# A diffusion-backbone layer on one core: TensorE in a hand-written, software-pipelined order from the step sums to the out-projection

## The chip, the cores and the metric

The kernel runs on one core of one Trainium2 chip. Its engines are PE (TensorE, matrix products), PEld (TensorE's weight load, which overlaps PE), DVE (VectorE), ACT (ScalarE), POOL (GpSimd) and SP (SyncE), which in this kernel only issues transfers. Each engine takes its instructions from a queue of its own, in order; semaphores hold an instruction back until what it reads is there. The metric is the device time of one execution in microseconds (us). A time "at 127.2" is counted from the start of the profiled span.

## The reference, cut to what matters

One layer over 256 noised tokens `x` and 256 context tokens `ctx`, both 1024 wide, float32 throughout. Both are normalised and modulated and go through one in-projection; the latent tokens pass a two-direction Mamba-2 scan that starts from the context's final state, and beside it a short gated convolution; both meet in the out-projection. A top-4-of-32 mixture of experts follows.

```python
mod_x = (jax.nn.silu(c) @ w_mod[i] + b_mod[i]).reshape(b, N_MOD, 1, D_MODEL)
hx = modulate(rmsnorm(x, norm1_g[i]), mod_x[:, 0], mod_x[:, 1])
proj = h @ w_in                                        # 1024 -> 5664 columns: z, x, B, C, dt, sc_b, sc_c, sc_u
xbc = jax.nn.silu(conv_seq(proj[..., X0:DT0], ssd_conv_w) + ssd_conv_b)
...
y, hf, hb = ssd_bidir(xs, bm, cm, dt_f, dt_b, a_f, a_b, d_skip, h0_f, h0_b)
y_ssd = group_rmsnorm(y.reshape(b, l, D_SSD) * jax.nn.silu(z), ssd_norm_g, SSD_GROUPS)
y_sc = sc_b * sc_conv(sc_c * sc_u, sc_conv_w)
out = jnp.concatenate([y_ssd, y_sc], axis=-1) @ w_out
...
x = x + mod_x[:, 2] * ox
x = x + mod_x[:, 5] * moe(modulate(rmsnorm(x, norm2_g[i]), mod_x[:, 3], mod_x[:, 4]), *moe_w)
```

`ssd_chunked` works in two chunks of 128 tokens: inside a chunk each head's output is (scores x decays) times the inputs, and the state carried in is added with its own decay.

## The kernel before, in words

**Numbers.** A float32 product is made from a high and a low part of each factor, both in the type fp32r: `split` copies the high part on ACT (`hi`) and subtracts for the low part (`lo`) on DVE or POOL, and `gemm` issues three products per row block of 128 (lines L292, L293, L295). A block of `proj` has 24 matmuls, 512 columns wide where latent and context tokens go together (X), 256 wide for the latent tokens alone (C, SC, SU, SB, Z). Each pair of blocks has one weight tile of 1 MB, which `load_cols` fetches (L223, tiles `wiX`, `wiC`, ...) into a ring of three slots (`RA`).

**Stages.** Up to 60 us: modulation of phase 0, norms, transposes, the B block and the first X blocks. Then:

- 60 to 127 us: the X blocks (2 to 7) and the C blocks, each followed by a depthwise convolution and SiLU on ACT and DVE. Beside them the step sums: `pds` (PE), then on DVE `dtx`, the running sums `acs` and `wc` (L431 to L453). `pc` (L460) turns these to token order, six small transposes, and DVE copies them into `dtc`. `px` (L501) transposes each X block, and DVE multiplies with `dtc` into `xdt` and `ws`. `decay_rows` splits the sums into the rows of `a4` on DVE (L487, L489). The four context states `pst` (L535), copied by ACT into `h0`, and the scores `pcb` (L544) end the stage.
- 127 to 187 us: the scan, 16 steps (8 head pairs `hp`, 2 directions `d_`). A step makes two decay tiles `rb` in PSUM (L565, L568; two buffers), ACT takes three exponentials of each (L572 to L576), DVE multiplies by the scores (`mx`), POOL by C (`ex`), and PE adds six products into `py` (L583, L586, L590), a tile of 64 output columns per head.
- 187 to 284 us: the short-conv blocks SC, SU, SB (24) and the gate blocks Z (8).
- 284 to 341 us: the out-projection, 192 matmuls (L825 to L827) into four PSUM tiles `po`; its weights `wo` are split on the way into `oh` and `ol`. `group_norm` (POOL, L671) makes the gated and normed `y` that the last half of the products needs. Then the router and, to the end, the 32 experts, whose weights (`gu`, `dn`, 1 MB a transfer, 384 of them) pass through 17 slots: `ringa` (3), `ringm` (2), `ringb` (5), six more, and one of another tile.

**Modulation on the side.** Phases 1 and 2 (`m1`, `m2`) are generators of 8 small steps (`pmod`, L202: one 1 MB tile `wm` against the conditioning vector, four products side by side in 32-column tiles of the array) and a final part of 16 tiny and 2 wide products (`pq`, `pgate`, L210, L216). Their tiles pass through `ringm`, two slots (`RM`).

**Order.** The program is written with a tile framework. A scheduler that works from modelled costs sets each engine's order, and so PE's; the code's order only fixes what depends on what. `tc.issue_after` holds an instruction behind another one.

Of the kernel before, what the change touches and what calls it, by code (L numbers as in the profile page):

```python
# [8 lines left out]
F32 = mybir.dt.float32  # L9
# [53 lines left out]
def body(ctx, tc, x, ctx_in, vectors_in, w_mod, b_mod, w_in, w_out, w_router, b_router, w_gate_up, b_gate_up,  # L63
# [128 lines left out]
    def mods(ph, gate, gate_first, col):  # L192
# [6 lines left out]
        for k in range(KD):  # L199
            w = load_mod(ph, k)  # L200
            for j in range(4):
                nc.tensor.matmul(acc[32 * j:32 * j + 32, :], ct[:, k, :], w[:, 512 * j:512 * j + 512],  # L202
                                 start=(k == 0), stop=(k == KD - 1), skip_group_check=True)
            yield
        nc.vector.tensor_add(rows, rows, acc)
# [196 lines left out]
    nc.tensor.matmul(pds, sdt.rearrange("p d h -> p (d h)"), dq, start=True, stop=True)  # L402
    se.close()

# [3 lines left out]
    for g in range(2):  # L408
        pp = pps[g]
        b = t2a.tile([P, 2, T], F32, name=f"b{g}")  # L410
        conv_silu(pp, 8 + g, 512, b)
        pb = ps.tile([P, 512], F32, tag="misc", bufs=2, name=f"pb{g}")
        for i in range(NT):
            nc.tensor.transpose(pb[:, i * P:(i + 1) * P], b[:, 1, i * P:(i + 1) * P], ident)
        nc.vector.tensor_copy(bcT[:, :, g, :], pb[:, :T].rearrange("p (i n) -> p i n", i=NT))
        bch.append(b)
# [40 lines left out]
    pc = ps.tile([P, 512], F32, tag="misc", bufs=2, name="pc")  # L457
    for i in range(NT):
        for w_, src in enumerate((dtx[:, :T], wc, acs)):
            nc.tensor.transpose(pc[:, (w_ * 2 + i) * 64:(w_ * 2 + i + 1) * 64], src[:, i * P:(i + 1) * P],  # L460
                                ident[0:H2, 0:H2])
    dtc = t2a.tile([P, 3, NT, 64], F32, name="dtc")
    nc.vector.tensor_copy(dtc[:, 0:2], pc[:, 0:256].rearrange("p (a b c) -> p a b c", a=2, b=2))
    steps_done = nc.vector.tensor_scalar(dtc[:, 2], pc[:, 256:384].rearrange("p (b c) -> p b c", b=2), -1.0, None, op0=ALU.mult)
# [27 lines left out]
    for q in range(4):  # L492
        wv = load_cols(X0 + 256 * q, f"X{q}") if q else None
        for half in range(2):
            ti = 2 * q + half
            pp = proj(wv, half, 512, f"X{ti}", nc.gpsimd) if q else pps[2 + half]
            cx = t2a.tile([P, 512], F32, tag="cx", bufs=2, name=f"cx{ti}")
            conv_silu(pp, ti, 512, cx.rearrange("p (m t) -> p m t", m=2), weighted.ins if ti else None)
            px = ps.tile([P, 512], F32, tag="misc", bufs=2, name=f"px{ti}")
            for i in range(4):  # L500
                nc.tensor.transpose(px[:, i * P:(i + 1) * P], cx[:, i * P:(i + 1) * P], ident)  # L501
            nc.gpsimd.tensor_scalar(yb[:, ti, :], cx[:, :T], vec("d", ti), None, op0=ALU.mult)

            for s_, dst in enumerate((xdt, ws)):
                for i in range(NT):
                    nc.vector.tensor_mul(
                        dst[:, :, i, 2 * ti:2 * ti + 2, :],
                        dtc[:, s_, i].rearrange("p (d h) -> p d h", d=2)[:, :, 2 * ti:2 * ti + 2, None]
                        .to_broadcast([P, 2, 2, HD]),
                        px[:, (2 * s_ + i) * P:(2 * s_ + i + 1) * P].rearrange("p (h q) -> p h q", h=2)[:, None]  # L510
                        .to_broadcast([P, 2, 2, HD]))
            if ti == 1:
                decay_rows()
            if ti >= 4:
                with tc.issue_after(steps_done.ins):
                    next(m1)


    t2s = sa.enter_context(tc.tile_pool(name="t2s", bufs=1, reuse_waits="tile"))
    cch = []  # L520
    wv = load_cols(C0, "C")
    for g in range(2):
        pp = proj(wv, g, T, f"C{g}")
        cc = t2s.tile([P, T], F32, name=f"c{g}")
        last_silu = conv_silu(pp, 10 + g, T, cc[:, None, :])
        cch.append(cc)
# [4 lines left out]
    for g in range(2):  # L531
        for d_ in range(2):
            pst = ps.tile([P, 512], F32, tag="misc", bufs=2, name=f"pst{d_}{g}")
            for i in range(NT):
                nc.tensor.matmul(pst, bcT[:, i, g, :], ws[:, d_, i, 8 * g:8 * g + 8, :],  # L535
                                 start=(i == 0), stop=(i == NT - 1))
            nc.scalar.copy(h0[d_][g], pst)


    cb = [[None, None], [None, None]]  # L540
    for g in range(2):
# [12 lines left out]
    for hp in range(8):  # L554
        py = ps.tile([P, T], F32, tag="py", bufs=1, name=f"py{hp}")
        g = hp // 4
        for d_ in range(2):
            ja, jb = (0, 1) if d_ == 0 else (1, 0)
            half = slice(P, T) if d_ == 0 else slice(0, P)
            xd = xdt[:, d_]  # L560
            mxs, exs = [], []
            for h_ in (2 * hp, 2 * hp + 1):
                row = 32 * d_ + h_
                pr = ps.tile([P, 4, P], F32, tag="rb", bufs=2, name=f"rb{h_}_{d_}")
                nc.tensor.matmul(pr, selr[:, row:row + 1].to_broadcast([P, P]), a4, start=True, stop=False,  # L565
                                 skip_group_check=True)
                for blk in (0, 2) if d_ == 0 else (1, 2):
                    nc.tensor.matmul(pr[:, blk, :], identb, maskf if d_ == 0 else maskb, start=False,  # L568
                                     stop=(blk == 2), skip_group_check=True)
                mx = t2s.tile([P, 384], F32, tag="mx", bufs=4, name=f"mx{h_}_{d_}")  # L570
                with tc.issue_after(last_silu):
                    nc.scalar.activation(mx[:, 0:256], pr[:, 0:2, :].rearrange("p a b -> p (a b)"), AF.Exp,  # L572
                                         bias=dtc[:, 2, ja, row:row + 1])
                    nc.scalar.activation(mx[:, 256:384], pr[:, 2, :], AF.Exp, bias=dtc[:, 2, jb, row:row + 1])
                    ex = t2s.tile([P, 2, P], F32, tag="ex", bufs=4, name=f"ex{h_}_{d_}")
                    nc.scalar.activation(ex, pr[:, 3:0:-2, :] if d_ == 0 else pr[:, 0:4:3, :], AF.Exp)  # L576
                nc.vector.tensor_mul(mx, mx, cb[g][d_])
                exf = ex.rearrange("p a b -> p (a b)")
                nc.gpsimd.tensor_tensor(exf, exf, cch[g], op=ALU.mult)
                mxs.append(mx)  # L580
                exs.append(exf)
            for hh in range(2):
                nc.tensor.matmul(py[64 * hh:64 * hh + 64, :], xd[:, ja, 2 * hp + hh, :], mxs[hh][:, 0:256],  # L583
                                 start=(d_ == 0), stop=False, skip_group_check=True)
# [778 lines left out]
```

## Time and profile before

| | before |
|---|---|
| median of 3 runs | 1318.14 us (1315.64 to 1318.76) |
| the profiled execution's own time | 1318.35 us |
| its span | 1316.6 us |
| PE busy | 1186.5 us, 90% of the span |
| PEld, DVE, ACT, POOL busy | 41%, 33%, 20%, 11% |
| mean granted clock of PE | 0.963 |
| moved by DMA | 466 MB |

The profiled execution has 1.75 us outside the span that the trace covers. PE's busy share counts matmuls as they lie in its pipeline, so it does not tell how tightly they follow each other; for that the starts of successive matmuls are read.

### The profile page before, as it was taken

How to read it: one execution, taken by the hardware profiler on the slowest of the kernel's cores; microseconds unless marked ns; L12 is line 12 of the kernel's file. 1: busy time of each engine (PE TensorE's matmuls, PEld its weight loads, DVE VectorE, ACT ScalarE, POOL GpSimd, SP SyncE). 2: the span in 40 equal slices, each digit the busy share in tenths (PEclk: the TensorE clock that was granted, in tenths of full speed). 3: DMA queues.
4: the chain of work that ended last, by engine and by line, in shares of the span. 5: the costliest groups of instructions: out<-in, count | busy, mean ns of one | idle time of the engine just before them, and what ended most of it. 6: DMA issues, size and time to landing. Idle time of an engine off the chain costs nothing.

```text
span 1316.6 us, 16133 instructions
## 1 busy us (share of the span) xinstructions
PE 1186.5 (90%) x6105; PEld 543.7 (41%) x6105; DVE 428.9 (33%) x874; ACT 259.1 (20%) x509; POOL 139.0 (11%) x147
## 2 busy tenths in 40 slices
PE   7989999999899988899988879998987899888984
PEld 6666479977633332244223213432321243223221
DVE  5475344553523432222223212222321213212222
ACT  5445454435410010010001001000100010001002
POOL 1232454405300100000000000000000000000001
PEclk9989999999899999999999978999998999899997
DMA  9725439785599999999999999999999999999994
GB/s 324 258 96 160 160 94 318 233 327 209 217 371 416 416 416 415 415 415 416 417 417 415 416 416 417 417 416 414 415 416 417 416 417 416 416 417 417 416 416 161
DMA packets 111841, 466.12 MB, mean 354 GB/s; under 512 B 9576, under 2 KB 40424, under 8 KB 76944
## 3 DMA queue, kind: packets, MB, share of 16 engines
q1 hardware_dynamic: 111504, 464.37, 88.9%
q8 instruction: 50, 0.82, 0.3%
q0 software_dynamic: 256, 0.67, 0.1%
q14 instruction: 31, 0.25, 0.1%
HBM read 463.97 MB, written 1.05 MB: 353 GB/s over the span
## 4 chain that ended last, share of the span: by engine, by line
PE 57%; DMA 12%; DVE 6%; ACT 1%; issue 1%; POOL 0%; ACTq 0%; DVEq 0%; SPq 0%; POOLq 0%
PE pdn L1051 8%; DMA gu<-in_w_gate_up_dram 8%; PE pg L1039 7%; PE pl L1039 6%; PE pg L1109 6%; PE pc L1015 6%; PE pgl L1080 5%; DMA dn<-in_w_down_dram 5%; PE pdn L1093 4%; PE pdn L1116 3%; PE pd L927 2%; PE pgl L1074 1%; PE pat L1008 1%; DVE ye L1062 1%; PE po L827 1%; PE po L825 1%
## 5 line engine op out<-in xcount | busy, mean ns | idle before, releaser
L1039 PE MATMUL pg<-gu,xe 128*64 128x512 f32 x480 | 151.0, 603 | 2.2 <-DMA gu<-in_w_gate_up_dram 2.0
L1039 PE MATMUL pl<-gu,xe 128*64 128x512 f32 x480 | 148.0, 593 | 0.0
L982 ACT ACTIVATE s<-a 128x512 f32<-128x512 f32 (+1 forms) x35 | 19.1, 545 | 589.6 <-DVE a L981 589.6
L1080 PE MATMUL pgl<-gu,xe 128*32 128x512 f32 x896 | 115.9, 622 | 15.3 <-DMA gu<-in_w_gate_up_dram 15.3
L1015 PE MATMUL pc<-ye,gt 64*128 64x512 f32 (+1 forms) x256 | 101.5, 640 | 28.7 <-DVE ye L1062 14.7
L1051 PE MATMUL pdn<-dn,at 128*64 128x512 f32 x480 | 118.5, 640 | 6.9 <-ACT at L1010 6.8
L1017 DVE TENSOR_TENSOR x<-x,pc 128x512 f32<-128x512 f32 x128 | 84.4, 685 | 119.4 <-PE pc L1015 119.4
L981 DVE TENSOR_SCALAR a<-pg 128x512 f32<-128x512 f32 x21 | 14.5, 691 | 217.3 <-PE pg L1039 151.8
L1109 PE MATMUL pg<-gu,xe 128*128 128x512 f32 x192 | 83.9, 592 | 0.0
L1231 POOL DMA_DIRECT2D fg<-in_final_g_dram x1 | 0.6, 591 | 746.6 <-PE pd L927 746.6
L1015 PEld LDWEIGHTS pc<-ye,gt 64*128 64x128 f32 (+1 forms) x256 | 29.2, 185 | 101.1 <-DVE x L1017 45.5
L1093 PE MATMUL pdn<-dn,at 128*32 128x512 f32 x448 | 65.7, 696 | 5.4 <-ACT at L1010 5.4
L1062 DVE TENSOR_TENSOR ye<-g2s,pdn 128x512 f32<-128x512 f32 x29 | 19.9, 688 | 154.4 <-PE pdn L1051 107.6
L1039 PEld LDWEIGHTS pl<-gu,xe 128*64 128x64 f32 x480 | 41.8, 137 | 65.8 <-issue 65.5
L1039 PEld LDWEIGHTS pg<-gu,xe 128*64 128x64 f32 x480 | 38.2, 136 | 71.2 <-issue 57.4
L1051 PEld LDWEIGHTS pdn<-dn,at 128*64 128x64 f32 x480 | 34.2, 146 | 73.7 <-issue 57.6
L1080 PEld LDWEIGHTS pgl<-gu,xe 128*32 128x32 f32 x896 | 24.7, 111 | 91.4 <-issue 50.0
L1109 PEld LDWEIGHTS pg<-gu,xe 128*128 128x128 f32 x192 | 35.8, 190 | 41.6 <-issue 40.9
L927 PE MATMUL pd<-oh,hr 128*128 128x256 f32 (+1 forms) x256 | 41.9, 305 | 5.6 <-DVE xe L929 5.0
L1116 PE MATMUL pdn<-dn,at 128*128 128x512 f32 x96 | 43.5, 601 | 0.0
L927 PEld LDWEIGHTS pd<-oh,hr 128*128 128x128 f32 x256 | 34.1, 198 | 20.9 <-DVE xe L929 10.7
L995 DVE TENSOR_SCALAR go<-io,gp 128x128 f32<-128x128 f32 x56 | 18.6, 370 | 68.9 <-PE pgo L999 68.9
(398 smaller groups left out, 1678.7 us busy)
## 6 DMA issues: line engine op xcount, KB each, us to landing
gu<-in_w_gate_up_dram SPq DMA_DIRECT2D x256, 1024.0 KB, 19.9
dn<-in_w_down_dram SPq DMA_DIRECT2D x127, 1024.0 KB, 20.0
wm<-in_w_mod_dram SPq DMA_DIRECT2D x16, 1024.0 KB, 5.0
wim<-in_w_mod_dram SPq DMA_DIRECT2D x8, 1024.0 KB, 11.6
wo<-in_w_out_dram SPq DMA_DIRECT2D x8, 1024.0 KB, 6.9
wiX<-in_w_in_dram SPq DMA_DIRECT2D x4, 1024.0 KB, 10.6
wiSC<-in_w_in_dram SPq DMA_DIRECT2D x4, 1024.0 KB, 8.0
wiSU<-in_w_in_dram SPq DMA_DIRECT2D x4, 1024.0 KB, 6.4
```

The source lines that it names most:

```text
L927: nc.tensor.matmul(pd[:, :width], hr[n // 2][:, n % 2, k * P:(k + 1) * P], oh[:, n % 2, :], start=(n == 0), stop=(n == 3))
L982: nc.scalar.activation(s, a, AF.Sigmoid, scale=ALPHA)
L995: nc.vector.tensor_scalar(go if cap == P else go.rearrange("p (a s) -> p a s", s=cap), io1 if cap == P else io1[:, None, 0:cap].to_broadca ...
L1015: nc.tensor.matmul(pc_, lhs, rhs, start=True, stop=True)
L1017: return nc.vector.tensor_add(ysl, ysl, pc_).ins
L1039: nc.tensor.matmul(pp[64 * hf:64 * hf + 64, :], xk[k], gu[k][:, i * FF + hf * 512:i * FF + hf * 512 + 512], start=False, stop=(k == KD - 1 ...
L1051: down = nc.tensor.matmul(pdn[64 * hf:64 * hf + 64, :], at[:, kk % 4, 64 * (kk // 4):64 * (kk // 4) + 64], dn[kk // 2][:, (kk % 2) * D + h ...
L1062: nc.vector.tensor_mul(ye, g2s, pdn)
L1080: nc.tensor.matmul(pgl[32 * q:32 * q + 32, :], xk[k], gv[:, :, 256 * q:256 * q + 256], start=False, stop=(k == KD - 1), skip_group_check=True)
L1093: down = nc.tensor.matmul(pdn[j:j + 32, :], at[:, c2, 32 * q:32 * q + 32], dn[q][:, c2 * D + hf * 512:c2 * D + hf * 512 + 512], start=(q = ...
L1109: nc.tensor.matmul(pgs[i][hf], xk[k], gu[k][:, i * FF + hf * 512:i * FF + hf * 512 + 512], start=False, stop=(k == KD - 1))
L1116: nc.tensor.matmul(pdn, ats[kk // 4][:, kk % 4, :], dn[kk // 2][:, (kk % 2) * D + hf * 512:(kk % 2) * D + hf * 512 + 512], start=(kk == 0) ...
```

## The change: what it does

PE's order from `pds` to the last matmul of the out-projection is taken from the code (`tc.manual_schedule` for this one engine); the other engines' orders are still set by the scheduler. The code is cut into functions, and a written sequence calls them.

```diff
+    in_order = ExitStack()
+    in_order.enter_context(tc.manual_schedule(engines={mybir.EngineType.PE}))
+    with tc.issue_after(last[0]):
+        nc.tensor.matmul(pds, sdt.rearrange("p d h -> p (d h)"), dq, start=True, stop=True)
...
+    def c_block(g):
+        if g == 0:
+            wcol["C"] = load_cols(C0, "C")
+        pp = proj(wcol["C"], g, T, f"C{g}", nc.vector)
...
+    x_block(0)
+    x_block(1)
+    x_block(2)
+    context_b(0)
+    context_b(1)
+    x_block(3)
+    c_block(0)
+    for _ in range(3):
+        next(m1)
+    token_steps()
+    x_tokens(0)
+    x_tokens(1)
+    decay_rows()
+    c_block(1)
+    x_block(4)
+    x_tokens(2)
+    x_tokens(3)
+    x_block(5)
+    x_tokens(4)
+    for d_ in range(2):
+        context_state(d_, 0)
+    x_block(6)
+    x_tokens(5)
+    scores(0)
+    last_silu = x_block(7)
+    x_tokens(6)
+    scores(1)
+    for _ in range(2):
+        next(m1)
+    x_tokens(7)
+    sc_steps = [(kind, 2 * q + half) for q in range(4) for kind in "CUB" for half in range(2)]
+    fill = [lambda: context_state(0, 1), lambda: context_state(1, 1)]
+    fill += [lambda a=a: sc_block(*a) for a in sc_steps[:12]]
+    step = decays(0)
+    for s_ in range(16):
+        if fill:
+            fill.pop(0)()
+        if s_ >= 2:
+            next(m1 if s_ < 6 else m2, None)
+        done_ = step
+        if s_ < 15:
+            step = decays(s_ + 1)
+        outputs(s_, *done_)
...
+    sc_parts()
+    for a in sc_steps[12:]:
+        sc_block(*a)
+        sc_parts()
...
-        if n_ in (1, 2):
-            group_norm(n_ - 1, rgs[n_ - 1])
-        if n_ == 3:
+        if n_ in (2, 3):
+            group_norm(n_ - 2, rgs[n_ - 2])
+        if n_ == 4:
             bgr = router_operands()
...
+    in_order.close()
```

`token_steps` is the old code of `pc` and `dtc`, `x_tokens` that of `px`, `xdt` and `ws`, `context_state` that of one `pst`, `scores` that of one `pcb`, `decays` and `outputs` are the two halves of a scan step, and `sc_block` is one SC, SU or SB block. The products themselves stay as they were. The low parts of C1 and of the odd SU blocks move from POOL to DVE. In a generator's last step the addition of `pmod` to `rows` now stands before the yield. Transfers change their order on SP with all this; the two loads of `x2` (L806), which stood ahead of three weight transfers late in the out-projection, now follow all of `wo` and `gu0`.

Three places of the engines' orders follow; a name with a number behind its last underscore is one buffer, and "x8" stands for eight alike. The first place is PE around `pc`, the transposes of the step sums. Before, they stand inside block X4:

```order
L295 MATMUL ppX3_726<-hhi_188,loX3_723 128x512 x8
L292 MATMUL ppX4_773<-hhi_188,hiX4_769 128x512
L293 MATMUL ppX4_773<-hlo_189,hiX4_769 128x512
L292 MATMUL ppX4_773<-hhi_188,hiX4_769 128x512
L460 MATMUL pc_613<-ident_82,wc_604 128x64
L460 MATMUL pc_613<-ident_82,acs_603 128x64
L460 MATMUL pc_613<-ident_82,dtx_585 128x64
...
L293 MATMUL ppX4_773<-hlo_189,hiX4_769 128x512
```

After the change they stand behind the first C block and three steps of modulation phase 1 (`wm1_0` to `wm1_2`):

```order
L296 MATMUL ppC0_725<-hhi_188,loC0_722 128x256 x8
L202 MATMUL pmod1_756<-wm1_0_760,ct_169 32x512 x4
L202 MATMUL pmod1_756<-wm1_1_766,ct_169 32x512 x4
L202 MATMUL pmod1_756<-wm1_2_772,ct_169 32x512 x4
L470 MATMUL pc_778<-ident_82,dtx_582 128x64
L470 MATMUL pc_778<-ident_82,wc_601 128x64
L470 MATMUL pc_778<-ident_82,acs_600 128x64
```

What moved: a whole block and three modulation steps now stand between X3 and `pc`, and nothing of X4 stands before it.

The second place is PE in the scan. Before, a step's products into `py1` (heads 2 and 3, forward) lie split around the next step's decay tiles `rb2_1` and `rb3_1` and one quarter of a modulation step:

```order
L202 MATMUL pmod1_814<-wm1_5_1272,ct_169 32x512
L565 MATMUL rb2_1_1185<-a4_630,selr_102 128x512
L583 MATMUL py1_1156<-mx2_0_1161,xdt_629 64x256
L568 LDWEIGHTS identb_84
...
L565 MATMUL rb3_1_1196<-a4_630,selr_102 128x512
L568 LDWEIGHTS identb_84
L568 MATMUL rb3_1_1196<-maskb_88,identb_84 128x128
L583 MATMUL py1_1156<-mx3_0_1172,xdt_629 64x256
L586 MATMUL py1_1156<-mx2_0_1161,xdt_629 64x128
...
L590 MATMUL py1_1156<-ex2_0_1164,h000_1054 64x256
```

After the change, step 3 (heads 2 and 3, backward) reads:

```order
L296 MATMUL ppSC1_1252<-hhi_188,loSC1_1249 128x256 x8
L202 MATMUL pmod1_756<-wm1_6_1279,ct_169 32x512 x4
L574 MATMUL rb4_0_1285<-a4_618,selr_102 128x512
...
L574 MATMUL rb5_0_1296<-a4_618,selr_102 128x512
...
L604 MATMUL py1_1241<-mx2_1_1223,xdt_617 64x256
L604 MATMUL py1_1241<-mx3_1_1234,xdt_617 64x256
L607 MATMUL py1_1241<-mx2_1_1223,xdt_617 64x128
L607 MATMUL py1_1241<-mx3_1_1234,xdt_617 64x128
L611 MATMUL py1_1241<-ex2_1_1226,h010_621 64x256
L611 MATMUL py1_1241<-ex3_1_1237,h010_621 64x256
```

What moved: a whole short-conv block (here SC1) and a whole modulation step stand in each step, the next step's two decay tiles follow, and this step's products come last, all six together.

The third place is SP, which issues the transfers, at the start of the X blocks. Before:

```order
L223 DMA wiX1_675<-in_w_in_dram 128x8x256
L223 DMA wiX2_767<-in_w_in_dram 128x8x256
L189 DMA wm1_0_818<-in_w_mod_dram 128x2048
L189 DMA wm1_1_869<-in_w_mod_dram 128x2048
L223 DMA wiX3_875<-in_w_in_dram 128x8x256
L223 DMA wiC_982<-in_w_in_dram 128x8x256
L223 DMA wiSC0_1607<-in_w_in_dram 128x8x256
L189 DMA wm1_2_922<-in_w_mod_dram 128x2048
```

After:

```order
L224 DMA wiX1_637<-in_w_in_dram 128x8x256
L224 DMA wiC_719<-in_w_in_dram 128x8x256
L189 DMA wm1_0_760<-in_w_mod_dram 128x2048
L189 DMA wm1_1_766<-in_w_mod_dram 128x2048
L224 DMA wiX2_852<-in_w_in_dram 128x8x256
L224 DMA wiX3_961<-in_w_in_dram 128x8x256
L189 DMA wm1_2_772<-in_w_mod_dram 128x2048
L189 DMA wm1_3_1071<-in_w_mod_dram 128x2048
```

What moved: `wiC` comes second instead of fifth, and `wm1_2`, which takes the slot of `wm1_0`, comes straight behind the X tiles.

## Rows read from the trace of the kernel before

**Rows 1.** Page, section 2: GB/s moved, span in 40 slices.

```profile
GB/s 324 258 96 160 160 94 318 233 327 209 217 371 416 416 416 415 415 415 416 417 417 415 416 416 417 417 416 414 415 416 417 416 417 416 416 417 417 416 416 161
```

**Rows 2.** Window: length; busy PE, PEld, DVE, ACT, POOL; PEclk, DMA share, GB/s.

```profile
346.00:364.00 18.00, 14.61 (x75) 9.27 (x73) 10.83 (x38) 7.77 (x20) 1.80 (x2) 0.81 0.02 5
```

**Rows 3.** SP queue's waits: line, releaser: us in total, times, longest us.

```profile
SPq L728 <- PE pl L1039: 80.4, 42, 22.0
```

**Rows 4.** Windows of the four stages from step sums to out-projection.

```profile
60.20:127.20 67.00, 62.07 (x298) 44.51 (x298) 42.37 (x85) 33.18 (x48) 21.15 (x16) 0.95 0.44 141
127.20:187.30 60.10, 60.10 (x376) 32.41 (x375) 24.05 (x47) 32.38 (x97) 26.91 (x32) 1.00 0.27 88
187.30:284.10 96.80, 96.80 (x793) 89.02 (x793) 46.95 (x68) 40.29 (x54) 35.10 (x21) 1.00 0.84 283
284.10:340.90 56.80, 53.08 (x245) 42.88 (x244) 24.26 (x46) 27.42 (x52) 28.13 (x25) 0.97 0.73 287
```

**Rows 5.** Timeline, PE, X blocks: start us, us, instruction, [idle before <-releaser].

```profile
71.33 0.24 PE L460 MATMUL pc<-ident,dtx 64*128 64x64 f32 x1 [1.46 <-DVE dtx L433]
...
79.21 0.37 PE L460 MATMUL pc<-ident,wc 64*128 64x64 f32 x1 [3.39 <-DVE wc L453]
```

**Rows 6.** Windows: two stretches behind a wait of PE.

```profile
79.20:85.50 6.30, 6.29 (x23) 5.10 (x23) 5.22 (x17) 0.00 (x0) 0.76 (x1) 0.50 0.50 163
293.50:297.90 4.40, 4.36 (x17) 3.66 (x17) 0.96 (x4) 1.86 (x3) 0.56 (x1) 0.61 0.80 337
```

**Rows 7.** The modulation tiles `wm` (16 transfers of 1 MB), their landing.

```profile
DMA to landing us min/median/max: 4.8/5.0/7.1
```

**Rows 8.** Timeline, PE, scan (start us, us).

```profile
133.23 0.50 PE L565 MATMUL rb<-a,selr 128*128 128x512 f32 x1
...
134.21 1.04 PE L202 MATMUL pmod<-wm,ct 128*32 128x512 f32 x2
...
143.64 0.74 PE L583 MATMUL py<-mx,xdt 128*64 128x256 f32 x4
...
144.96 0.49 PE L565 MATMUL rb<-a,selr 128*128 128x512 f32 x1
```

**Rows 9.** Timelines, POOL in that scan step, ACT and DVE at a Z block.

```profile
135.04 1.83 POOL L579 TENSOR_TENSOR ex<-ex,c 128x256 f32<-128x256 f32 x2 [3.97 <-ACT ex L576]
...
276.43 1.05 ACT L286 CAST hiZ<-wiZ 128x1024 fp32r<-128x1024 f32 x1 [1.48 <-PE ppZ L293]
...
277.51 1.23 DVE L287 TENSOR_TENSOR loZ<-wiZ,hiZ 128x1024 fp32r<-128x1024 f32 x1 [1.32 <-ACT hiZ L286]
```

**Rows 10.** Timeline, PE, short-conv blocks.

```profile
188.29 0.28 PE L292 MATMUL ppSU<-hhi,hiSU 128*128 128x256 f32 x1
...
191.17 0.28 PE L292 MATMUL ppSU<-hhi,hiSU 128*128 128x256 f32 x1
...
197.02 1.06 PE L202 MATMUL pmod<-wm,ct 128*32 128x512 f32 x8
198.01 0.38 PE L292 MATMUL ppSB<-hhi,hiSB 128*128 128x256 f32 x1
```

**Rows 11.** Groups by line and shape, PE, 127.2 to 187.3: busy us, mean ns.

```profile
L565 PE MATMUL rb<-a,selr 128*128 128x512 f32 x30 | 13.8, 468 | 0.0
...
L202 PE MATMUL pmod<-wm,ct 128*32 128x512 f32 x32 | 8.4, 605 | 0.0
L293 PE MATMUL ppSC<-hlo,hiSC 128*128 128x256 f32 x16 | 4.9, 324 | 0.0
...
L216 PE MATMUL pgate<-rows,ident 128*128 128x512 f32 x4 | 2.2, 627 | 0.0
L210 PE MATMUL pq<-ident,rows 128*128 128x1 f32 x16 | 1.9, 251 | 0.0
```

**Rows 12.** Timeline, PE, out-projection's two waits.

```profile
293.54 0.88 PE L827 MATMUL po<-ol,sc 128*128 128x512 f32 x2 [1.79 <-DVE ol L689]
...
311.06 0.50 PE L827 MATMUL po<-ol,sc 128*128 128x512 f32 x1 [1.93 <-POOL ol L689]
```

More of the change, by code (lines that the diff above doesn't have):

```diff
@@ L490, in decay_rows @@
                                              a4[r0:r0 + 32, blk].bitcast(F32))
[L492 to L516, printed above, removed]
@@ L519, in body, with x_block @@
[L519 to L526, printed above, removed]
+    cx = {}
+    wcol = {}
+    def x_block(ti):
+        q, half = ti // 2, ti % 2
+        if q and not half:
+            wcol["X"] = load_cols(X0 + 256 * q, f"X{q}")
+        pp = proj(wcol["X"], half, 512, f"X{ti}", nc.gpsimd) if q else pps[2 + half]
+        cx[ti] = t2a.tile([P, 512], F32, tag="cx", bufs=2, name=f"cx{ti}")
+        silu = conv_silu(pp, ti, 512, cx[ti].rearrange("p (m t) -> p m t", m=2), weighted.ins if ti else None)
+        nc.gpsimd.tensor_scalar(yb[:, ti, :], cx[ti][:, :T], vec("d", ti), None, op0=ALU.mult)
+        return silu
@@ L529, in body @@
+    cch = [None, None]
+    def c_block(g):
+        if g == 0:
+            wcol["C"] = load_cols(C0, "C")
+        pp = proj(wcol["C"], g, T, f"C{g}", nc.vector)
+        cch[g] = t2s.tile([P, T], F32, name=f"c{g}")
+        conv_silu(pp, 10 + g, T, cch[g][:, None, :], weighted.ins)
     h0 = [[t2a.tile([P, 512], F32, tag=("hf", "dr")[d_], bufs=2, name=f"h0{d_}{g}") for g in range(2)]
           for d_ in range(2)]
[L531 to L537, printed above, removed]
@@ L540, in body, with context_state, scores @@
-    cb = [[None, None], [None, None]]
-    for g in range(2):
+    def context_state(d_, g):
+        pst = ps.tile([P, 512], F32, tag="misc", bufs=2, name=f"pst{d_}{g}")
+        for i in range(NT):
+            nc.tensor.matmul(pst, bcT[:, i, g, :], ws[:, d_, i, 8 * g:8 * g + 8, :],
+                             start=(i == 0), stop=(i == NT - 1))
+        nc.scalar.copy(h0[d_][g], pst)
+    cb = [None, None]
+    def scores(g):
         pcb = ps.tile([P, 512], F32, tag="misc", bufs=2, name=f"pcb{g}")
@@ L552, in body, with decays @@
         cb[g] = (f, b)
-    for hp in range(8):
-        py = ps.tile([P, T], F32, tag="py", bufs=1, name=f"py{hp}")
+    def decays(s_):
+        hp, d_ = s_ // 2, s_ % 2
         g = hp // 4
[L557 to L584, printed above, removed]
-            for hh in range(2):
-                nc.tensor.matmul(py[64 * hh:64 * hh + 64, half], xd[:, jb, 2 * hp + hh, :], mxs[hh][:, 256:384],
-                                 start=False, stop=False, skip_group_check=True)
-            for hh in range(2):
-                h_ = 2 * hp + hh
-                nc.tensor.matmul(py[64 * hh:64 * hh + 64, :], h0[d_][g][:, (h_ % 8) * HD:(h_ % 8 + 1) * HD], exs[hh],
-                                 start=False, stop=(d_ == 1), skip_group_check=True)
-        nc.vector.tensor_add(yb[:, hp, :], yb[:, hp, :], py)
-        if hp % 2 == 0:
-            next(m1)
@@ L595, in body @@
[L595 to L610 removed]
+        ja, jb = (0, 1) if d_ == 0 else (1, 0)
@@ L614, in body @@
-        for half, ti in enumerate(tis):
-            pp = proj(wv, half, T, f"SU{ti}")
+        elif kind == "U":
             nc.vector.tensor_mul(cs[ti], cs[ti], pp[:, :T])
@@ L702, in body @@
             nc.vector.tensor_mul(yb[:, ti, :], yb[:, ti, :], z)
-        next(m2)
     squares = [group_squares(g) for g in range(2)]
```

124 lines of the change are left out of this document (90 added, 34 removed).

## The prediction, made before the changed kernel ran

> **What bounds the kernel now.** I start at the end and go back. In the slices of the page the bytes moved stand at 414 to 417 GB/s from the thirteenth slice to the last but one [rows 1]: from about 365 us on the experts take their weights as fast as they come. Before that the transfers stand still: 5 GB/s from 346 to 364 us [rows 2]. The queue of SP tells why. It has a weight tile to fetch but no slot: its longest wait, 22.0 us, is for expert 0's first products (`pl`) [rows 3], which let the first slot go. All slots are full by 346 us, so what the transfers do before that cannot move the end; what moves it is when PE comes to expert 0. That follows the router, and the router follows the last out-projection matmul at 340.9. So a microsecond taken from PE's path up to 340.9 is a microsecond at the end, as long as the slots are still full when expert 0 starts.
>
> Then the four stages of that path [rows 4]. The busy share would mislead: PE is busy 60.1 of 60.1 us in the scan and 96.8 of 96.8 in the short-conv stage, but its weight load is busy 32.41 in the one and 89.02 in the other. The scan is full of matmuls that wait for each other's pipeline, not of work. So I compare each stage's length with its instructions at the start-to-start price that they have where they run densely.
>
> **Prices.** A 256-wide block takes 2.88 us (188.29 to 191.17), a modulation step 0.99 (197.02 to 198.01), and the first matmul after such a step is listed 0.10 longer than its like in a dense run [rows 10]. A step's two decay tiles take 0.98 (133.23 to 134.21), its products in one piece 1.32 (143.64 to 144.96) [rows 8].
>
> **The change part by part.**
>
> *X and C blocks, 67.0 us.* Now lost: PE waits 1.46 us for `dtx` and 3.39 for `wc` at `pc` [rows 5], and behind the second wait runs 6.3 us at a granted clock of 0.50, the lower level (1.2 instead of 2.4 GHz) [rows 6], which costs half of that, 3.1. Together 7.95. The new order gives all of this back, since C0 and three modulation steps stand between X3 and `pc`, and `wc` is ready by then. But it brings a wait of its own: `wm1_2` takes the slot of `wm1_0` and can only be fetched when the first modulation step is through. Its landing takes 5.0 us at the median, 4.8 at least, 7.1 at most [rows 7]; one step of 0.99 covers a part, 4.1 with 0.1 for the queue is left. Nothing else may run: behind the waiting product PE's fixed order holds `pc`, on which `dtc`, `xdt` and `ws` depend. So PE stands idle about as long as before, and I put down the same lower clock behind it, 3.1. `px1` comes close behind `pc` and needs its PSUM buffer (two of that tag) back, which DVE frees after other work: 0.9, my estimate. In sum 8.1 instead of 7.95, a loss of 0.15. The bounds: without the clock's fall 3.1 better, with a landing of 7.1 some 2.1 worse. That C's transfer comes ahead of X2's costs nothing: X1 covers it.
>
> *Scan, 60.1 us.* At the prices it holds 15 pairs of decay tiles (30 listed [rows 11], two a step), 14.7; 16 steps of products, 21.1; 4 modulation steps (32 listed, 8 a step), 4.0; phase 1's final part, 1.9 + 2.2 = 4.1; and 40 listed matmuls of SC blocks (16 with `hlo` [rows 11], as many with `hhi`, 8 with `lo`) at 0.12, 4.8. That makes 48.7, so 11.4 us are lost. The order shows where: the products of a step are cut into pieces around the next step's decay tiles, and modulation steps are cut too, with little dense work between. In the changed order whole blocks of 2.88 lie between, and a full step is 2.88 + 0.99 + 0.98 + 1.32 = 6.2 us. What could still be lost: the first states of group 1 wait for the last `ws` (about 1.1, three DVE products at the head), the last step has no block before it (1.0), and entering 12 blocks from the narrower tiles costs 12 x 0.11 = 1.3. Together 3.4, a gain of 8.0. The two ends are 11.4 (nothing lost) and below zero (third rival).
>
> The Trainium skill, "TensorEngine Tiling (Array Packing)", Key Properties, speaks against this: a change of tiling mode, not merely of tile, drains TensorE. Priced as the tail of a listed matmul beyond its pitch (0.28 - 0.12 = 0.16) on the way into and out of 12 blocks, the switches would be 3.9 instead of 1.3 and the time 2.6 later; the row with 0.10 decides for the smaller price.
>
> *Short-conv and Z blocks, 96.8 us.* Twelve SC blocks and all of `m2` leave for the scan; the rest keeps its density (89.02 us of weight load). The moved work keeps its price, so this comes to nothing. The low parts that go from POOL to DVE lie beside a PE that is never waiting there: nothing too; without that cover each would hold up what is behind it on DVE by its length, 1.23 [rows 9].
>
> *Out-projection, 56.8 us.* Lost now: 1.79 waiting for DVE's `ol`, 1.93 for POOL's [rows 12], and 1.7 by the clock of 0.61 in the 4.4 us behind the first [rows 6]; 5.4. After the change phase 2's final part no longer stands between the last Z block and the first out-projection matmuls, so the first two splits of `wo` have less time: 2.0 of waiting, about as the 1.79 now. `group_norm` comes one row later, and POOL, which makes `y` and `ol`, is less crowded: 0.8 for 1.93. The clock I put at 1.0. Together 3.8, a gain of 1.6; the bounds are 5.4 (no gain) and 0.
>
> *Transfers.* `x2` no longer blocks the queue ahead of three weight tiles. That queue is waited for nowhere late, since all slots fill before expert 0 starts; nothing.
>
> **The sum.** -8.0 - 1.6 + 0.15 = -9.4. The profiled execution took 1318.35 us, 0.2 above the median of 1318.14; so 1308.9 on its scale, **1308.7** on the median's. The out-projection's last matmul should come at 331.5 instead of 340.9.
>
> **The rivals.**
>
> *Better.* The wait for `wm1_2` does not lower the clock (-3.1) and the out-projection loses nothing (-3.8): 1301.8, and a little less where the scan loses less than 3.4. For it: PE does work nearly up to that wait. Against it: both waits of over 1.7 us here were followed by a low clock in [rows 6].
>
> *Nothing arrives.* Either the scan cannot be made denser because PE is busy all through, or expert 0 finds its slots unfilled. By the first, -1.6 + 0.15 gives 1316.7; by the second, the transfers stay the bound and the time stays at 1318. For the first speaks the busy time; against it the weight load, and the price of 1.32 that some steps reach. Against the second speak 18 us without transfers; a start 9.4 earlier still leaves 8.6.
> The Trainium skill, "Perfetto Trace Analysis", Identifying the Most-Contended Engine, says that matmul busy share is no good measure of the room left and LDWEIGHTS busy share is; by that rule the scan has room, as the sum has it.
>
> *Slower.* In the fixed order each step ends with products that need ACT's exponentials, DVE's `mx` and POOL's `ex`. If these are late, everything behind them waits, where before the scheduler had put something else. The point: 14 steps have a full or near-full filling; at 9.4/14 = 0.67 us of waiting in each the gain is gone, at 0.96 the kernel is 4 us slower, at 1.2 it takes 1325.5. Against it: from the first decay matmul at 133.23 to the end of POOL's second product at 136.87 (135.04 + 1.83) the chain took 3.6 us [rows 8, 9], and a step offers 6.2 - 1.3 = 4.9 before its own products come round. For it: ACT also makes a high part per block and DVE a low part (1.05 and 1.23 [rows 9]), which stand in the same queues and can push the chain to about 4.6; only 0.3 is then left.
>
> **How the numbers follow.** The forecast (1303 to 1313.5) 0.62, better 0.16, nothing arrives 0.11, slower 0.11. About 0.3%, 4 us, is what a measurement of this kernel tells from no change. Faster than 1314.2: the forecast, the better case and 0.01 of the slower one, whose waits may be small: 0.79. Within 4 us: nothing arrives and 0.01 of the slower one, 0.12. Slower: 0.09. The range from 1299.5 to 1317 leaves out the slower case, half of the second half of "nothing arrives", and a little below. The likeliest case's own range is 1303 to 1313.5: the unknown clock (3.1), the landing (2.1) and the out-projection's waits (up to 3.8) on either side.
>
> **What would show it.** Right: the last out-projection matmul near 331.5, and transfers without bytes for 8 to 9 us less; a scan from about 124 to 220 us with steps of 6.2 and hardly an idle PE; `pc` without a wait for `wc`, but a wait of some 4 us at `pmod` for a transfer, ahead of it. Wrong: waits of PE for `mx` or `ex` at each step's products; a granted clock at the lower level in the scan; a transfer as the releaser of expert 0's first products; a wait for `wi` tiles in the scan, should `wm` hold them up in the queue.

## The result, and the profile after

| | before | after |
|---|---|---|
| median | 1317.54 us (4 runs) | **1299.60 us** (4 runs, 1299.11 to 1302.23) |
| ratio, 95% interval | | **0.9869** (0.9851 to 0.9887) |
| span of the profiled execution | 1316.6 us | 1297.7 us |
| last out-projection matmul starts | 340.92 us | 324.71 us |

The kernel is 17.9 us faster. The forecast was 1308.7 with a range down to 1299.5: the direction held, the forecast gain was about half of what came, and the measured time lies 0.1 us inside the lower end of the range. That it lies inside is luck: the likeliest case had a range of its own down to 1303 only, and the case called "better" had 1301.8.

The end first. Windows of the changed kernel (stretch, length; busy PE, PEld, DVE, ACT, POOL; granted clock, DMA share, GB/s): its transfers stand still as those of before did [rows 2], from about 330 to 347, and start again when expert 0 lets slots go. Then SP's longest wait, which answers to [rows 3] (times as there):

```profile
329.50:347.10 17.60, 14.22 (x81) 8.88 (x75) 11.04 (x39) 8.23 (x21) 1.87 (x2) 0.90 0.04 13
```

```profile
SPq L799 <- PE pl L1111: 83.8, 43, 20.8
```

The slots are full before expert 0 starts in both kernels, so the end still hangs on PE's path. The three later stages of that path, as windows of the changed kernel (scan, remaining short-conv and Z blocks, out-projection), answer to [rows 4]:

```profile
123.53:218.45 94.92, 93.88 (x715) 63.71 (x713) 48.44 (x77) 49.80 (x124) 36.24 (x41) 1.00 0.67 226
218.45:276.14 57.69, 57.69 (x481) 57.69 (x481) 33.12 (x45) 27.42 (x37) 15.79 (x12) 1.00 0.75 247
276.14:324.94 48.80, 48.12 (x226) 39.23 (x224) 23.53 (x43) 25.32 (x50) 27.92 (x26) 1.00 0.80 310
```

The second row is the one to look at: 20 blocks in 57.69 us, 2.88 each, and the weight load is busy in all of it. In the scan, a full step on PE's timeline (start, length):

```profile
137.11 0.49 PE L574 MATMUL rb<-a,selr 128*128 128x512 f32 x1
...
138.08 0.65 PE L604 MATMUL py<-mx,xdt 128*64 128x256 f32 x4
138.56 0.39 PE L607 MATMUL py<-mx,xdt 128*64 128x128 f32 x4
138.78 0.60 PE L611 MATMUL py<-ex,h 128*64 128x256 f32 x4
...
142.38 1.07 PE L202 MATMUL pmod<-wm,ct 128*32 128x512 f32 x8
143.37 0.49 PE L574 MATMUL rb<-a,selr 128*128 128x512 f32 x1
```

From 137.11 to 143.37 are 6.26 us, the forecast step of 6.2. All six products (each listed twice, as float32) stand in one piece. Ahead of the scan the wait that the prediction put there is in place, and what it did to the clock; PE's timeline, then the window behind the wait:

```profile
76.00 1.93 PE L202 MATMUL pmod<-wm,ct 128*32 128x512 f32 x16
82.28 1.93 PE L202 MATMUL pmod<-wm,ct 128*32 128x512 f32 x8 [4.35 <-DMA wm<-in_w_mod_dram]
84.14 0.37 PE L470 MATMUL pc<-ident,dtx 64*128 64x64 f32 x1
```

```profile
82.20:87.60 5.40, 5.32 (x27) 3.41 (x28) 4.26 (x9) 1.38 (x3) 0.69 (x1) 0.50 0.92 311
```

`pc` itself waits for nothing now. In the out-projection the two waits of [rows 12] have shrunk to about a fifth and a seventh:

```profile
280.20 0.50 PE L898 MATMUL po<-ol,sc 128*128 128x512 f32 x1 [0.34 <-DVE ol L761]
...
297.62 0.50 PE L898 MATMUL po<-ol,sc 128*128 128x512 f32 x1 [0.26 <-POOL ol L761]
```

### The profile page after: what moved, and what is told of

Its sections match the earlier page's. It is cut to its first block, busy times and chain, and to the rows that moved or that the text cites. A ratio compares the mean times of both kernels' runs of the same rounds, so it can differ in the third digit from the quotient of the medians.

```text
span 1297.7 us, 16107 instructions
## 1 busy us (share of the span) xinstructions
PE 1169.8 (90%) x6105; PEld 537.8 (41%) x6105; DVE 437.0 (34%) x879; ACT 258.1 (20%) x509; POOL 124.7 (10%) x142
## 4 chain that ended last, share of the span: by engine, by line
PE 75%; DMA 15%; DVE 6%; ACT 1%; issue 1%; SPq 1%; POOL 0%; ACTq 0%; DVEq 0%; POOLq 0%
PE pdn L1123 8%; DMA gu<-in_w_gate_up_dram 8%; PE pg L1111 7%; PE pl L1111 7%; PE pg L1181 6%; PE pc L1087 6%; PE pgl L1152 6%; DMA dn<-in_w_down_dram 5%; PE pdn L1188 3%; PE pdn L1165 3%; PE pd L999 2%; DMA wim<-in_w_mod_dram 2%; PE pgl L1146 2%; PE pat L1080 1%; PE ppX L293 1%; PE ppX L294 1%
## 5 line engine op out<-in xcount | busy, mean ns | idle before, releaser
L1152 PE MATMUL pgl<-gu,xe 128*32 128x512 f32 x896 | 115.9, 627 | 11.4 <-DMA gu<-in_w_gate_up_dram 11.4
```

What stands on the lines that cost most here:

```text
L1152: nc.tensor.matmul(pgl[32 * q:32 * q + 32, :], xk[k], gv[:, :, 256 * q:256 * q + 256], start=False, stop=(k == KD - 1), skip_group_check=True)
```

## The experiments

The theory was that PE's path had become denser, for the reasons of the sum, and that the end follows it one to one. Its rivals were that the moved transfers or the cut-up code brought the gain, and, part by part, that another wait would come where one was taken away. Times are medians; each has its own runs of the kernel before beside it (1317 to 1318.5).

**Does the end follow PE's path?** Work was put in that nobody uses.

```diff
+    idle = ps.tile([P, 512], F32, tag="py", bufs=1, name="idle")
+    for i in range(84):
+        nc.tensor.matmul(idle[:, :T], hhi[:, i % KD, 0:P], hhi[:, i % KD, :T], start=(i == 0), stop=(i == 83))
```

> The change with 84 more matmuls of 256 columns (10.1 us by the block's price of 0.12 each) behind the last short-conv block; their result is not used. Theory (the end moves one to one with PE's path, since every slot for expert weights is full before expert 0 starts): last out-projection matmul and device time both 9 to 11 us later, 1308.5 to 1311. Rival (the transfers are the bound already and part of the gain came from elsewhere): time less than 6 us later, under 1306.

1309.34 us, 9.7 more than the change. In the profiled executions the last out-projection matmul (333.44 instead of 324.71) and the time (1308.28 instead of 1299.57) are both 8.7 later: the end follows PE one to one. The 8.7 is a little under the 9 to 11 expected, because in this run the scan began 1.3 us earlier (122.2 instead of 123.5). The run shows what a delay of PE costs; that a further saving is also worth its length is shown by the last run on the X stage below, up to its 6.7 us and no further.

**Is it the written order?** The one line that takes PE from the scheduler was left out; the code's sequence stayed.

```diff
-    in_order.enter_context(tc.manual_schedule(engines={mybir.EngineType.PE}))
```

> The changed code cut into functions as it is, but without the written order: the scheduler sets PE's order again. Theory (the written order makes PE dense): the cut products in the scan return, the out-projection's last matmul comes at 333 to 341 us instead of 324.9, and the time is 1308 to 1318. Rival (the moved transfers and the regrouped code bring the gain): both stay near the change, last matmul 325 to 328, time 1300 to 1303.

1298.11 us (ratio to before 0.9853, 0.9836 to 0.9869), the last out-projection matmul at 324.05. My theory fell here: the order need not be written. Given this code, the scheduler comes to nearly the same order by itself; a step of this run on PE's timeline:

```profile
136.69 0.49 PE L573 MATMUL rb<-a,selr 128*128 128x512 f32 x1
...
137.66 0.65 PE L603 MATMUL py<-mx,xdt 128*64 128x256 f32 x4
...
141.95 1.06 PE L202 MATMUL pmod<-wm,ct 128*32 128x512 f32 x8
142.95 0.49 PE L573 MATMUL rb<-a,selr 128*128 128x512 f32 x1
```

It takes 6.26 too (136.69 to 142.95), with its products in one piece. Two runs with the written order for a part only say the same.

> The written order ends with the scan; the scheduler orders the short-conv, Z and out-projection matmuls. Theory: those stages are dense by themselves once modulation is gone from them, so the last out-projection matmul stays within 1.5 us of 324.9 and the time at 1299 to 1302. Rival (the written order is what took the waits out of the out-projection): waits of 2 to 4 us come back there, time 1302 to 1305.

1300.74 us, last matmul at 325.08.

> The written order begins only with the scan's first decays; the scheduler orders the X and C blocks. Theory (the X stage nets nothing, its losses are 9.7 before and about 9 after): scan still starts at 122 to 127 us, steps of 6.2 us, time 1298 to 1303. Rival (the X stage's order is part of the gain, since the scan needs its operands early): scan starts 4 us or more later, time 1304 or more.

1301.92 us, 325.19. The X stage, left to the scheduler, has another wait for the same loss: 3.92 us for a convolution (`cv`) ahead of the second C block. So the gain lies in what the code now says, not in who orders PE. What of it?

**The blocks among the scan steps?** First the written order with a bare scan: blocks and modulation steps behind it.

```diff
-        if fill:
-            fill.pop(0)()
-        if s_ >= 2:
-            next(m1 if s_ < 6 else m2, None)
+        if s_ < 2:
+            fill.pop(0)()
...
+    while fill:
+        fill.pop(0)()
+        next(m1, None)
+    for _ in range(9):
+        next(m2, None)
```

> Written order as in the change, but the scan bare: no short-conv block and no modulation step between its decays and its products; they follow behind the scan. Theory (the blocks inside the scan hide the chain decays, exponentials, mx and ex): a step is 2.3 us of PE and its chain 3.6, PE waits 0.7 to 1.3 us for mx or ex in most of 16 steps, last out-projection matmul at 335 to 345 us, time 1309 to 1319. Rival (cutting the products in pieces was the loss, and whole products are enough): no such waits, last matmul 325 to 328, time 1299 to 1303.

1327.59 us, slower than before, but not for the reason that I gave. Between the start of one step's decays and the next (134.85 to 164.61, 12 steps) a step takes 2.48 us where its work is 2.30: the scan loses 0.2 a step. The loss stands behind it, where the modulation steps follow each other and each waits for its tile (a window, and two of six such rows of PE):

```profile
216.00:243.00 27.00, 15.84 (x66) 5.11 (x67) 1.02 (x3) 0.00 (x0) 0.00 (x0) 0.52 0.85 307
```

```profile
216.72 1.71 PE L202 MATMUL pmod<-wm,ct 128*32 128x512 f32 x8 [4.49 <-DMA wm<-in_w_mod_dram]
...
225.16 1.94 PE L202 MATMUL pmod<-wm,ct 128*32 128x512 f32 x8 [3.94 <-DMA wm<-in_w_mod_dram]
```

The six waits make 14.1 us (4.49, 0.86, 3.94, 1.48, 1.68, 1.67), and the granted clock is at 0.52 there. This run mixes two things, so the next leaves the modulation steps in the scan and takes only the blocks out.

> Modulation steps stay in the scan, one a step; the 12 short-conv blocks stand behind it. The bare scan lost little in itself, but its modulation steps stood together and waited for their 5 us transfers. Theory (the blocks are not needed to hide the exponentials, the modulation steps only to be spread): waits of PE in scan under 0.5 us a step, time 1299 to 1304, unless two slots for the modulation tiles can't bring one every 3.3 us, then waits for wm of 1 to 2 us a step. Rival (only the blocks hide the chain): waits for mx or ex in most steps, 1306 or more.

1299.10 us; the scan's last products start at 181.09 and the last out-projection matmul at 322.47. Behind the scan's head PE waits once, 0.35 for `mx` in the last step. The blocks hide nothing that needs hiding. The modulation steps need their distance. The same bare scan left to the scheduler:

> The same code with the bare scan, but PE's order left to the scheduler. Theory A (the scheduler follows the order in which the code is written): it leaves the scan nearly bare or puts in fragments, time 1308 to 1319 as with the written bare order or as in the kernel before. Theory B (the scheduler finds the filling by itself and the new functions only gave it the decays one step ahead): time 1298 to 1303.

1302.18 us, 325.15: the time of theory B with the order of theory A. The scan stays nearly bare and ends at 169 (13 listed matmuls of blocks and one modulation step lie in it); what the scheduler does is to keep the last modulation steps apart, between the blocks behind the scan, where PE waits for none of them:

```profile
215.40 1.07 PE L202 MATMUL pmod<-wm,ct 128*32 128x512 f32 x8
...
218.86 1.07 PE L202 MATMUL pmod<-wm,ct 128*32 128x512 f32 x8
...
222.32 1.06 PE L202 MATMUL pmod<-wm,ct 128*32 128x512 f32 x8
```

So neither the blocks nor the modulation steps have to stand in the scan.

**Decays a step ahead?** What is left in the scan is that each step's decays are written ahead of the products of the step before. This was undone, with the scheduler, whose order else gave 1298.11.

```diff
-        done_ = step
-        if s_ < 15:
-            step = decays(s_ + 1)
-        outputs(s_, *done_)
+        outputs(s_, *decays(s_))
```

> Order left to the scheduler, code as in the change, but each step's decays are written directly ahead of its own products instead of one step ahead. Theory (decays one step ahead in the code are what made the scan dense; the kernel before lacked that): products come cut around the next decays again, scan 5 to 10 us longer, time 1304 to 1312. Rival (it is the blocks and modulation steps written among the scan steps): time 1298 to 1302.

1311.60 us (ratio 0.9952, 0.9936 to 0.9968), last matmul at 335.95, 11.9 later than with the decays ahead. PE's timeline in a step of this run:

```profile
142.82 0.49 PE L573 MATMUL rb<-a,selr 128*128 128x512 f32 x1
...
144.91 0.65 PE L603 MATMUL py<-mx,xdt 128*64 128x256 f32 x2
145.48 0.39 PE L294 MATMUL ppSU<-hlo,hiSU 128*128 128x256 f32 x1
...
146.15 0.43 PE L603 MATMUL py<-mx,xdt 128*64 128x256 f32 x1
...
147.37 0.39 PE L294 MATMUL ppSU<-hlo,hiSU 128*128 128x256 f32 x1
...
149.88 0.49 PE L573 MATMUL rb<-a,selr 128*128 128x512 f32 x1
```

The products come in two pieces again, as in the kernel before: 0.57 (144.91 to 145.48) and 1.22 (146.15 to 147.37), 1.79, where the change takes 1.23 in one piece (138.08 to 139.31). The block around them is cut too, and each re-entry costs about 0.1: together the 0.8 by which a step is longer. The step takes 7.06 (142.82 to 149.88) instead of 6.26, without a wait. In five places of this scan PE also waits for `mx`, 3.2 us in all and 0.91 at most.

This run and the one with 1298.11 issue their transfers up to the scan in the same order and have the low parts on the same engines, so it is not these that make the 13.5 us between them. What they are worth by themselves was not run. Nor was the converse: the kernel before with nothing changed but its decays a step ahead.

**The X stage.** One modulation step fewer ahead of the transposes:

> Two modulation steps instead of three stand ahead of the step sums' transposes; the third goes to the two ahead of the scan. Theory A (the wait of 4.35 us for the third step's transfer and the low clock behind it are a loss of their own): the wait goes, the scan starts 5 to 6.5 us earlier, time 1293 to 1295. Theory B (DVE has the row casts, C1's low part and X3's convolution ahead of the copy of the step sums, in one unbroken run to 83.9 us, so the second X transpose waits for its buffer instead): a wait of 4 to 6 us at px, the scan starts 0 to 1.5 us earlier, time 1298 to 1300.

1307.72 us, slower than the change: theory B was right at its place (6.28, a little over its 4 to 6), and a second wait came that neither theory had. PE's timeline:

```profile
85.22 1.09 PE L519 MATMUL px<-ident,cx 128*128 128x128 f32 x4 [6.28 <-DVE dtc L473]
...
129.31 1.93 PE L202 MATMUL pmod<-wm,ct 128*32 128x512 f32 x8 [6.03 <-DMA wm<-in_w_mod_dram]
```

The third of the steps ahead of the scan needs the slot of the first, which starts at 121.35; its transfer is issued at 122.48, when that step is through. A first try to clear the way to `dtc` (its edit is part of the one below, with X4 ahead of C1):

> The change with the way to the step sums' copy cleared: two modulation steps ahead of the transposes, the third behind X4's tokens, DVE's row casts and C1 behind the copy, three convolution buffers instead of two, the step sums' PSUM tile taken from the outputs' tag, X4 ahead of C1. Theory (the X stage's 4.35 us wait and the low clock behind it hang on what stands ahead of that copy on ACT, DVE and in PSUM): no wait over 1.5 us before the scan's first decays, these come at 117 to 119.5 instead of 123.5, time 1293 to 1296. Rival (another wait takes its place, for X4's parts or the copy): decays at 122 or later, time 1298 or more.

1300.94 us, the rival. PE waits 1.84 us for `wc` and 3.55 for C1's low part. The first of these is a collision; DVE's and POOL's timelines:

```profile
72.92 2.88 DVE L452 TENSOR_TENSOR_SCAN acs<-one,da 32x256 f32<-32x256 f32 x1
75.81 0.68 DVE L453 TENSOR_TENSOR_SCAN acs<-one,da 32x256 f32<-32x256 f32 x1
```

```profile
72.87 2.39 POOL L288 TENSOR_TENSOR loX<-wiX,hiX 128x1024 fp32r<-128x1024 f32 x1 [9.97 <-ACT hiX L287]
```

A running sum of 0.68 us takes 2.88 when POOL has started a subtraction 0.05 us earlier, and ends 0.54 behind POOL's. The second try moves what collides:

```diff
-    for _ in range(3):
-        next(m1)
-    token_steps()
+    for _ in range(2):
+        next(m1)
+    steps = token_steps()
     x_tokens(0)
     x_tokens(1)
-    decay_rows()
     c_block(1)
     x_block(4)
     x_tokens(2)
     x_tokens(3)
+    next(m1)
     x_block(5)
     x_tokens(4)
-    for d_ in range(2):
-        context_state(d_, 0)
+    with tc.issue_after(steps):
+        decay_rows()
+    context_state(0, 0)
     x_block(6)
+    context_state(1, 0)
...
-        t = t2a.tile([P, m, T], F32, tag="cv", bufs=2, name=f"cv{ti}")
+        t = t2a.tile([P, m, T], F32, tag="cv", bufs=3, name=f"cv{ti}")
...
-        pc = ps.tile([P, 512], F32, tag="misc", bufs=2, name="pc")
+        pc = ps.tile([P, 512], F32, tag="py", bufs=1, name="pc")
...
+        with tc.issue_after(weighted.ins) if nm == "C1" else nullcontext():
+            nc.scalar.copy(hi, src)
```

C1's low part also goes to POOL, and the first two short-conv blocks stand ahead of the scan.

> The next try at the X stage: C1's high part behind the weighted sums' exponential and its low part on POOL, two modulation steps ahead of the transposes and the third behind X3's tokens, row casts last, three convolution buffers, the step sums' PSUM tile from the outputs' tag, the states of group 0 apart, two short-conv blocks ahead of the scan. Theory (what stood ahead of the copy of the step sums was the cause; in the first try C1's low part and a shared port took its place): no wait over 1.5 us before the scan, scan's end at 211 to 214, last out-projection matmul at 317 to 320, time 1292 to 1295. Rival (a wait comes back at another place): 1298 or more.

**1292.50 us** (1291.37 to 1294.34; ratio to before 0.9803, 0.9783 to 0.9823), faster than both kernels. The largest wait ahead of the scan is left at C1, and the window around it has the full clock:

```profile
82.97 1.22 PE L297 MATMUL ppC<-hhi,loC 128*128 128x256 f32 x8 [0.32 <-POOL loC L289]
```

```profile
78.00:86.00 8.00, 7.62 (x58) 5.97 (x48) 6.36 (x19) 6.68 (x10) 6.41 (x4) 1.00 0.62 191
```

The last out-projection matmul starts at 318.05, 6.7 ahead of the change's 324.71, and the time is 7.1 less. The scan ends later than I had put it (217, not 211 to 214), and two more blocks are done by then than in the change. The edit changes several things of the X stage at once; which of them the gain needs was not run.

**The out-projection.** Its head as before: phase 2's final part behind Z, `group_norm` and `router_operands` one row earlier.

> The change with the out-projection's head as before: phase 2's final part between Z and the out-projection, group norm at rows 1 and 2, router operands at row 3. Theory (the gain of some 4.5 us there comes from DVE's queue: the subtraction for the router's bias, written later, no longer stands ahead of the second low part of wo): a wait of 1 to 2 us for ol and low clock come back, last matmul at 327 to 330, time 1302 to 1305. Rival (the stage was late because POOL was crowded by what came before): no wait, time 1299 to 1301.

1303.24 us, last matmul at 328.33, 3.6 later. The size is as expected, the place only in part. PE's timeline:

```profile
276.84 0.50 PE L898 MATMUL po<-oh,sc 128*128 128x512 f32 x1 [0.68 <-ACT g L218]
281.11 0.50 PE L900 MATMUL po<-ol,sc 128*128 128x512 f32 x1 [0.79 <-DVE ol L762]
...
285.98 1.05 PE L738 MATMUL pr<-ident,rg 128*128 128x128 f32 x4 [1.53 <-DVE rg L732]
...
287.26 0.63 PE L899 MATMUL po<-oh,sc 128*128 128x512 f32 x1
```

The wait for `ol` is 0.79; another of 1.53 is for the norm's factor `rg`, which has no wait where `group_norm` stands a row later. Behind it the matmuls are listed at 0.63 instead of 0.39: the granted clock is 0.50 from 286.5 to 289.5. The edit undoes three things at once, and the waits tell them apart: 0.68 for `g` of the final part, 0.45 more than the change's 0.34 for `ol`, 1.53 for `rg` and about 1.5 by the clock.

In the kernel before, the wait for the second `ol` was 1.79, so one more thing was in it. DVE's and POOL's timelines, first of the kernel before, then DVE's of this run:

```profile
290.59 1.22 DVE L791 TENSOR_TENSOR bgr<-bg,bgr 64x1024 fp32r<-64x1024 f32 x1
291.85 1.64 DVE L689 TENSOR_TENSOR ol<-wo,oh 128x512 fp32r<-128x512 f32 x1
...
291.21 1.73 POOL L689 TENSOR_TENSOR ol<-wo,oh 128x512 fp32r<-128x512 f32 x1 [1.91 <-ACT oh L688]
```

```profile
280.37 0.69 DVE L762 TENSOR_TENSOR ol<-wo,oh 128x512 fp32r<-128x512 f32 x1
```

In both, DVE makes the router's low bias part `bgr` just ahead of `ol`. In the kernel before, this put `ol` behind the start of POOL's own `ol`, and it took 1.64 instead of 0.69, as the running sum did above; in this run POOL began 0.06 us behind DVE (280.43). The 0.95 is about the difference of the two waits.

## Why the prediction was right or wrong

**What bounds the kernel** held: the end follows PE up to expert 0. From the start of the last out-projection matmul to the end, the profiled executions of all fourteen kernels take 974.8 to 977.4 us, while that start lies between 318.05 and 352.68. One sign did not come: the standstill of the transfers was to shrink by 8 to 9 us, and is hardly shorter: 16.6 (330.2 to 346.8) after 18.1 (346.2 to 364.3). The prediction took the end of the filling as fixed; it moved with PE.

**The sum's terms**, each as stage length less work at the prediction's prices:

| term | forecast | measured |
|---|---|---|
| X and C blocks | 0.15 lost | about 0.1 gained |
| scan | 8.0 gained | 10.0 gained |
| short-conv and Z blocks | nothing | 1.4 gained |
| out-projection | 1.6 gained | 4.7 gained |

The scan: 36.8 for 16 steps, 34.6 for 12 blocks, 10.9 for 11 modulation steps, 7.0 for two final parts and 3.6 for two states make 92.9 of 94.92; 2.0 are lost, where 3.4 were forecast. A final part takes 3.5 from its start to the next matmul; the prediction's 4.1 added listed lengths, which overlap. With 3.5, the scan before held 48.1 of work and lost 12.0, not 11.4. The out-projection's stage was 56.8 with the 3.5 of a final part in it, 53.3 without, against 48.6 from 276.14 to the start of the last matmul. The short-conv stage held 30.3 blocks (87.4) and 8 modulation steps (7.9) in 96.8 and lost 1.5; it loses 0.1 now. The prediction put nothing there, though each modulation step between two blocks costs about 0.19 beyond its 0.99 (195.97 to 197.02 for eight matmuls of 0.12, and 198.01 to 198.24 for one): eight make the 1.5. The X stage's term is the remainder of the 16.2 by which the last matmul comes earlier, rounded. The other 2.7 of the span's 18.9 come behind it: some 1.2 before expert 0 (its first `pl` starts 17.4 earlier, at 343.11; the clock between router and expert was 0.66 in the ten us up to 361 and 0.81 in the nine up to 344), and 1.5 in the experts' stream, of which I can say only that medians of the kernel before differ by about as much from one set of runs to another.

**The step that failed** is the out-projection's term, short by 3.1: "so the first two splits of `wo` have less time: 2.0 of waiting", with 1.0 for the clock behind it. The opposite came: 0.34 of waiting, and a clock of 1.00 in the stage. I had looked at what PE would no longer cover, and not at DVE's queue, where the wait was made: `bgr` stood ahead of the second `ol` and put it into POOL's way. Where `router_operands` is written a row later, the scheduler puts `bgr` among the last short-conv blocks (251.1). The old head gave back 3.6 of the 4.7, but only 0.45 of that at `ol`, since there the collision did not come back; that `bgr` alone made the 1.79 is read from the timelines, and no run undid it by itself.

**The scan's mechanism** was right in what counted, the products in one piece and steps of 6.26; that whole blocks must lie between was not needed, since the bare scan takes 2.48 a step for 2.30 of work. Its size was short by 2.0. Entering a block costs what was forecast: a step's work is 6.17 at the prices, so 0.09 a step goes into the switches, 1.1 for twelve against 1.3. The ends cost less, 0.69 for `ws` at the head instead of 1.1 and 0.35 for `mx` at the last step instead of 1.0, and the loss before was larger by 0.6. The dearer price for the drain that the Trainium skill names ("TensorEngine Tiling (Array Packing)", Key Properties) would have made 24 x 0.16 = 3.8 of switches; the whole loss of the scan is 2.0, so the measured row decides for the small price.

**The X stage** came as written, with 4.35 for 4.1 of waiting, a clock of 0.50 behind it, and a sum near zero. The 0.9 for `px1` did not come; 0.96 for `ws` and 0.68 for `h` came elsewhere. The reason given for the clock, that "both waits of over 1.7 us here" were followed by a fall, left out the third such wait of [rows 12]: behind 1.93 at 311.06 the clock was 1.00 (311 to 316). That the wait can't just be taken away, since DVE's queue stands behind it, the prediction did not say; one run showed it.

**"Nothing arrives"** and **"Slower"** fell. The six products waited for `mx` once, 0.35 at the last step. The argument for that, a filling of 4.9 us against a chain of 3.6, was not the reason: with only the modulation steps between, or with nothing, PE still hardly waits (0.35 and 0.17 in the scan for `mx`). With the decays in the same step it waits five times for it, so it is the whole step of distance that hides the chain.

**What I gave as the cause** was too wide in one thing: I spoke of the fixed order. It is not needed; without it, the same code gives 1298.11.

## What to carry to other kernels

Where a loop step makes its operands on one engine and uses them on another, write the next step's operands ahead of this step's use: here 13.5 of 19.0 us hang on it (both runs in the scheduler's order), and the scheduler, given the code so, needs no written order. A product cut into pieces shows as PE busy without a wait; read it from the starts of matmuls and from the weight load's share. Before a wait is moved, read the queue of the engine that ends it: twice here the next work in that queue was the next wait, and once a wait of 1.79 shrank to 0.34 with a reordering that nobody meant for DVE.

## What the runs showed of the hardware

- A running sum on DVE with two inputs from SBUF took 2.88 us instead of 0.68 while POOL ran a subtraction of 2.39 us. This bears on the Trainium skill, "SBUF — State Buffer", SBUF: two separate sides: the port pair that the two engines share is held by one instruction until it ends. The trace agrees: POOL had started 0.05 us earlier, and 2.88 - 0.68 = 2.2 is about what was left of its 2.39. In the kernel before, a subtraction of 0.69 on DVE took 1.64 beside one on POOL that had started 0.64 earlier; the same one took 0.69 where it started 0.06 ahead of POOL's.
- The waits of over 4 us for a transfer were each followed by PE at the lower of its two levels (1.2 GHz): a granted clock of 0.50 for 5.4 us with the 4.35 here, 0.50 from 129 to 134 with the 6.03 of the run with one step fewer. Shorter waits went either way: behind 1.79 for `ol` 0.61 [rows 6] and behind 1.53 for `rg` 0.50, but behind 1.93 at 311.06 in the kernel before 1.00 (311 to 316), and behind 0.69 at the head of the scan 1.00.
- Modulation tiles of 1 MB, one directly behind another through two slots, held PE up for 14.1 us in six waits. In the run that left one in each step of 3.2 us (their products start at 147.91, 151.11, 154.32), PE waited 0.1 us for all of them together:

```profile
L202 PE MATMUL pmod<-wm,ct 128*32 128x512 f32 x88 | 11.7, 605 | 0.1
```
